# The tail of the last SSD group: the last y products in front of its four gate tiles, the norm's halves behind the second and the third

## The chip, the cores and the metric

The kernel runs on one core of one Trainium2 chip, as one program. The metric is the device time in microseconds of that core. Engines are named as in the profile: PE is TensorE's matmul, PEld its weight load, DVE is VectorE, ACT is ScalarE, POOL is GpSimd, SP is SyncE, which issues the DMAs. "L134" is line 134 of the kernel before; the lines up to 521 are the same in both versions.

## The reference, cut to what matters

One post-norm layer of a hybrid encoder on 512 tokens of width 1024, in float32. A combined projection makes, among others, z, x, B, C and dt for a bidirectional SSD branch, q, k and v for a dilated attention branch, and the logits of two gates. Both branches are projected, gated and merged:

```python
u = h @ w_in
z, xbc, dt_f_raw, dt_b_raw, q, k, v, gate_logits = jnp.split(u, ...)
y_ssd = ssd_branch(z, xbc, dt_f_raw, dt_b_raw, ...) @ w_proj_ssd
y_att = attention_branch(q, k, v) @ w_proj_attn
gates = jax.nn.sigmoid(gate_logits + b_gate).reshape(bsz, s, N_BRANCHES, D_MODEL)
mix = (gates[:, :, 0] * y_ssd + gates[:, :, 1] * y_att) @ w_out
h = layer_norm(alpha * h + mix, ln1_g, ln1_b)
```

The SSD branch has 4 groups of 8 heads of 64 channels. What matters here is its end, by group:

```python
y = y_f + y_b + d_skip[:, None] * xh
y = y.reshape(bsz, s, D_INNER) * jax.nn.silu(z)
yg = y.reshape(bsz, s, SSD_GROUPS, D_INNER // SSD_GROUPS)
yg = yg * lax.rsqrt(jnp.mean(jnp.square(yg), axis=-1, keepdims=True) + NORM_EPS)
return yg.reshape(bsz, s, D_INNER) * ssd_norm_w
```

A feed-forward sublayer follows.

## The kernel before, in words

Activations lie transposed: 128 channels on the partitions, 512 tokens along the free dimension. So the SSD output y is 16 tiles `ys[0..15]` of 128 x 512, four for each group. Large products are made in three passes of a split: a float32 operand is written as a high part (a cast to float32r on ACT) plus a low part (a subtraction on DVE), and `mm3` issues high x high, high x low, low x high (L134 to L136).

Weights come through a stream: a DMA on SP into one of three raw buffers (L87), the cast to `wh` on ACT (L108), the subtraction to `wl` on DVE (L109), two buffers of each. `ws.get()` hands out the next weight and prepares the one after it; casts and subtractions are issued with raised priority. A `wh` buffer comes free when PE has finished the tile before the one that runs.

The column tiles of the combined projection are tasks (`tile_task`, L288): 24 products of 128 x 128 with 128 x 512, then an eviction. Gate tiles "g0" to "g15" are evicted by ACT with a tanh (L314) and stored to DRAM by SP (L315).

In the SSD stage, `run` (L497) interleaves two generators by a budget of time: `ssd(g)`, the work of a group, and `bg(...)`, column tiles. This order is PE's own and is kept by hand (`manual_schedule` for PE); the other engines get their order from the framework's planner, which goes by priority, readiness and the tiles' buffers. In `ssd(g)` each pair of heads makes two masked matrices G on DVE (L462). The y products of a pair (`y_out`, L351) come one step later on PE: 8 products of G with x into `ps_y` (L358, 16 records in the profile), then yt on DVE (L360), an add on POOL (L361), the product with the gated z into `ys[j]` on DVE (L362), its square on ACT (L364), and a running sum of the squares on POOL (L366). The last pair of a group is left in `late` and is put out in the next group's start; for group 3 there is no next one.

The norm of a group, `norm(g)` (L335), is a generator in two halves. The first sums the squares over the channels by products with ones (`ps_ms`, L340), then takes the square root on ACT (L342; it needs a table of ACT that the tanh is not in) and the reciprocal on DVE (L343), into the small tile `rr`. The second spreads `rr` to all partitions by products (`ps_rr`, L347) and multiplies the group's four y tiles (L349 on DVE). Groups 0 to 2 have their norm inside the next group's `ssd`.

In group 3 there are 15 gate tiles, g1 to g15. The last four (`TAIL`), g12 to g15, are taken out of the interleaving and run behind it, with what is left of the group's y and norm between them (L522 to L529). Then the pools `sp` and `xp` of the SSD stage are closed (L530), and the projection stage opens its pools. `rr`, the x tiles, the squares and G lie in `sp`; the activations' split and the staging tiles of the gate stores lie in `xp`. The new right-side pools (for `yh`, the gates' loads and some attention tiles, `q` and `k` of the first pair among them) lie where `sp` was; the left-side ones (`mx`, `ap`, with `q` and `k` of the second pair) lie over `xp` as well. All 16 y tiles are split into `yh` (ACT, L560) and `yl` (DVE, L561), in order. The first projection tile (`ps_pa`, L134 to L136) takes y tiles 0 to 7; PE's order interleaves the projection with the attention branch, whose first scores (`ps_s`, L626) come after 18 products of the projection.

Of the kernel before, what the change touches and what calls it, by code (L numbers as in the profile page):

```python
# [43 lines left out]
def hybrid_layer_kernel(ctx: ExitStack, tc: tile.TileContext, t: dict, out: bass.AP):  # L44
# [103 lines left out]
    def ps_tile(tag, name, bufs):  # L148
        return psp.tile([P, 512], F32, name=name, tag=tag, bufs=bufs)
# [138 lines left out]
    def tile_task(kind, j):  # L288

        wh, wl = ws.get()  # L290
        ps = ps_tile("mm", f"ps_{kind}{j}", 3)
        for k in range(0, KT, 2):
            last_mm[0] = mm3(ps, [(wh[:, q * P:(q + 1) * P], wl[:, q * P:(q + 1) * P]) for q in (k, k + 1)], xs_hl[k:k + 2], k == 0, k == KT - 2)
            if k < KT - 2:
                yield QT
        evict(kind, j, ps)
        yield QT
# [29 lines left out]
    def bg(seq):  # L327
        for k, j in seq:
            yield from tile_task(k, j)
# [5 lines left out]
    def norm(g):  # L335

        sq = tail[g]
        ps = ps_tile("tp", f"ps_ms{g}", 3)
        for c in range(NCH):
            pe.matmul(ps[:, c:c + 1], sq[:, ch(c)], ones[:, 0:1], start=True, stop=True)  # L340
        rr = sp.tile([P, NCH], F32, name=f"rr{g}", tag="rr", bufs=1)
        act.activation(rr, ps[:, 0:NCH], AF.Sqrt, bias=epsv[:, 0:1], scale=1.0 / 512.0)  # L342
        dve.reciprocal(rr, rr)  # L343
        yield 6.0
        ps = ps_tile("tp", f"ps_rr{g}", 3)
        for c in range(NCH):
            pe.matmul(ps[:, ch(c)], rr[:, c:c + 1].to_broadcast([P, P]), ident, start=True, stop=True)  # L347
        for j in range(4 * g, 4 * g + 4):
            dve.scalar_tensor_tensor(ys[j], ys[j], vec[:, V_NW + j:V_NW + j + 1], ps, op0=ALU.mult, op1=ALU.mult)  # L349

    def y_out(g, pr, xt, ms, be, sqs):  # L351

        j = 4 * g + pr
        py = ps_tile("y", f"ps_y{j}", 2)
        for c in range(NCH):
            for hh in range(2):
                hs = slice((pr * 2 + hh) * HD, (pr * 2 + hh + 1) * HD)
                pe.matmul(py[hh * HD:(hh + 1) * HD, ch(c)], xt[c][:, hs], ms[hh][:, ch(c)], start=True, stop=True)  # L358
        yt = sp.tile([P, S], F32, name=f"yt{j}", tag="acc", bufs=2)
        dve.scalar_tensor_tensor(yt, fm["x", j], vec[:, V_DSK + j:V_DSK + j + 1], py, op0=ALU.mult, op1=ALU.add)  # L360
        pool.tensor_add(yt, yt, be[:, 0, :])  # L361
        dve.tensor_mul(ys[j], ys[j], yt)  # L362
        sq = sp.tile([P, S], F32, name=f"sq{j}", tag="sq", bufs=2)
        act.activation(sq, ys[j], AF.Square)  # L364
        if pr:
            pool.tensor_add(sq, sq, sqs[-1])  # L366
        sqs.append(sq)
        tail[g] = sq

    late = [None]  # L370
# [126 lines left out]
    def run(a, b, ta, tb):  # L497
        ua = ub = 0.0
        a, b = iter(a), iter(b)
        la = lb = True  # L500
        while la or lb:
            if la and (not lb or ua / ta <= ub / tb):
                try:
                    ua += next(a)
                except StopIteration:
                    la = False
            else:
                try:
                    ub += next(b)
                except StopIteration:  # L510
                    lb = False
# [6 lines left out]
    with tc.manual_schedule(engines={mybir.EngineType.PE}):  # L518
        for g in range(GROUPS):
            rest = len(mix[g]) - (TAIL if g == 3 else 0)  # L520
            run(ssd(g), bg(mix[g][:rest]), 86.5 if g else 93.5, 4 * QT * rest)
        nrm = norm(3)  # L522
        for n, (k, j) in enumerate(mix[3][rest:]):
            for _ in tile_task(k, j):
                pass
            if n == 0:
                y_out(*late[0])
            if n > 1:
                next(nrm, None)  # L529
    pa.close()  # L530

# [414 lines left out]
    for f in range(2):  # L946
# [21 lines left out]
        for c in range(2):  # L968
# [19 lines left out]
            for i in range(4):  # L988
# [5 lines left out]
                else:  # L994
                    n = 512 // len(pss[i])
# [72 lines left out]
```

## Time and profile before

| | |
|---|---|
| Median of 3 runs | 1033.44 us (1032.58 to 1034.84) |
| The profiled execution | 1033.47 us, span 1031.7 us |
| PE busy | 1017.8 us, 99% |
| DVE, ACT, POOL busy | 650.9, 501.7, 73.8 us |
| Mean granted TensorE clock | 0.997 |
| The tail with the four gate tiles on PE | 469.8 to 494.8 us of the span |

A row of a timeline gives start, duration, engine, line, operation, output and inputs, and in brackets the idle time of the engine before it with what ended it. Matmuls overlap: one is 0.39 us long and the next starts 0.23 us after it. A row of windows gives the stretch, its length, the busy time and the number of instructions of PE, PEld, DVE, ACT and POOL, the granted clock (1.00 is full), the share of the DMA engines and their rate in GB/s. A row of the waits gives who waited for whom, the total in us, how often, and the longest.

### The profile page before, as it was taken

Reading aid. Unit: us, or ns where it says so; the run is one execution under the profiler, and the core shown is the slowest. Engines: PE = TensorE matmul, PEld = TensorE weight load, DVE = VectorE, ACT = ScalarE, POOL = GpSimd, SP = SyncE. Lnnn points to the kernel's source line nnn. Section 1 sums busy time; section 2 is a strip of 40 time slices with the busy share of each in tenths; the row PEclk is TensorE's granted clock in tenths of the full one; section 3 lists DMA queues with packets and bytes.
Section 4 is the critical chain, followed back from the end, with each engine's and each line's share of the span. In section 5 each row is a group of like instructions: output and inputs, shape, how many; then the busy total and the mean of one; then the engine's idle time right before and its main releaser. Section 6 shows DMA issues by size and latency. Waiting matters only on the chain.

```text
span 1031.7 us, 13700 instructions
## 1 busy us (share of the span) xinstructions
PE 1017.8 (99%) x5169; PEld 843.1 (82%) x5169; DVE 650.9 (63%) x1035; ACT 501.7 (49%) x977; POOL 73.8 (7%) x66
## 2 busy tenths in 40 slices
PE   9999999999999999999899999999999999999997
PEld 7888888888878888888678788898888888888886
DVE  4296978689979996975786186744442324443346
ACT  4444877478758875764674353223432223433120
POOL 0000101221121022112000000000000000000000
PEclk9999999999999999999999999999999999999999
DMA  6445355425542554464753278212333333333322
GB/s 236 148 154 137 116 192 172 143 80 177 173 153 102 185 183 154 155 197 152 261 169 91 72 234 280 78 42 62 103 100 87 98 102 100 90 97 102 97 87 81
DMA packets 48449, 140.42 MB, mean 136 GB/s; under 512 B 6528, under 2 KB 7424, under 8 KB 48128
## 3 DMA queue, kind: packets, MB, share of 16 engines
q1 hardware_dynamic: 48240, 139.30, 42.5%
q8 instruction: 40, 0.66, 0.2%
q10 hardware_dynamic: 144, 0.26, 0.1%
q14 instruction: 25, 0.20, 0.1%
HBM read 128.25 MB, written 11.30 MB: 135 GB/s over the span
## 4 chain that ended last, share of the span: by engine, by line
PE 94%; DVE 3%; ACT 1%; DMA 1%; issue 1%; POOL 0%; DVEq 0%; ACTq 0%; POOLq 0%
PE ps_u L135 6%; PE ps_u L136 6%; PE ps_d L134 6%; PE ps_u L134 6%; PE ps_d L135 6%; PE ps_d L136 6%; PE ps_pa L134 3%; PE ps_g L134 3%; PE ps_pa L135 3%; PE ps_pa L136 3%; PE ps_g L136 3%; PE ps_g L135 3%; PE ps_z L134 3%; PE ps_z L135 3%; PE ps_z L136 3%; PE ps_x L134 3%
## 5 line engine op out<-in xcount | busy, mean ns | idle before, releaser
L109 DVE TENSOR_TENSOR wl<-wraw,wh 128x1024 fp32r<-128x1024 f32 (+1 forms) x165 | 201.0, 1222 | 239.0 <-ACT wh L108 234.2
L108 ACT CAST wh<-wraw 128x1024 fp32r<-128x1024 f32 (+1 forms) x165 | 171.2, 1041 | 266.5 <-PE ps_d L136 108.6
L135 PE MATMUL ps_u<-htl,wh 128*128 128x512 f32 (+1 forms) x288 | 105.3, 366 | 0.3 <-DVE htl L909 0.3
L134 PE MATMUL ps_u<-hth,wh 128*128 128x512 f32 (+1 forms) x288 | 105.3, 366 | 0.0
L136 PE MATMUL ps_u<-hth,wl 128*128 128x512 f32 (+1 forms) x288 | 105.2, 365 | 0.0
L135 PE MATMUL ps_d<-wl,fh 128*128 128x512 f32 (+1 forms) x272 | 102.5, 377 | 0.0
L134 PE MATMUL ps_d<-wh,fh 128*128 128x512 f32 (+1 forms) x272 | 102.4, 377 | 0.0
L136 PE MATMUL ps_d<-wh,fl 128*128 128x512 f32 (+1 forms) x272 | 102.4, 377 | 0.0
L135 PEld LDWEIGHTS ps_u<-htl,wh 128*128 128x128 f32 x288 | 54.3, 189 | 9.2 <-DVE htl L909 0.5
L134 PEld LDWEIGHTS ps_u<-hth,wh 128*128 128x128 f32 x288 | 54.2, 189 | 8.9 <-ACT hth L908 0.3
L136 PEld LDWEIGHTS ps_u<-hth,wl 128*128 128x128 f32 x288 | 54.3, 189 | 8.8
L136 PEld LDWEIGHTS ps_d<-wh,fl 128*128 128x128 f32 x272 | 51.2, 188 | 9.5
L134 PEld LDWEIGHTS ps_d<-wh,fh 128*128 128x128 f32 x272 | 51.2, 188 | 9.4
L135 PEld LDWEIGHTS ps_d<-wl,fh 128*128 128x128 f32 x272 | 51.2, 188 | 9.3
L134 PE MATMUL ps_pa<-yh,wh 128*128 128x512 f32 x128 | 52.9, 413 | 2.5 <-ACT yh L560 2.5
L135 PE MATMUL ps_pa<-yl,wh 128*128 128x512 f32 x128 | 50.8, 397 | 1.5 <-DVE yl L561 1.5
L134 PE MATMUL ps_g<-xh,wh 128*128 128x512 f32 x128 | 51.4, 401 | 0.0
L450 DVE SCALAR_TENSOR_TENSOR U<-bc,acr,U 128x128 f32<-128x128 f32 x128 | 45.8, 392 | 8.7 <-ACT U L448 8.7
L134 PE MATMUL ps_x<-xh,wh 128*128 128x512 f32 x128 | 50.9, 398 | 0.0
L134 PE MATMUL ps_z<-xh,wh 128*128 128x512 f32 x128 | 50.9, 398 | 0.0
L136 PE MATMUL ps_pa<-yh,wl 128*128 128x512 f32 x128 | 50.6, 396 | 0.0
L136 PE MATMUL ps_g<-xh,wl 128*128 128x512 f32 x128 | 50.0, 391 | 0.0
(262 smaller groups left out, 2184.2 us busy)
## 6 DMA issues: line engine op xcount, KB each, us to landing
wraw<-in_w_in_dram SPq DMA_DIRECT2D x68, 512.0 KB, 3.5
bc<-dr_acr SPq DMA_DIRECT2D x32, 512.0 KB, 4.2
wraw<-in_w_up_dram SPq DMA_DIRECT2D x32, 512.0 KB, 3.6
wraw<-in_w_dn_dram SPq DMA_DIRECT2D x32, 512.0 KB, 3.6
be<-dr_ear SPq DMA_DIRECT2D x32, 256.0 KB, 4.5
wraw<-in_w_ps_dram SPq DMA_DIRECT2D x16, 512.0 KB, 3.7
dr_gate<-g SPq DMA_DIRECT2D x16, 256.0 KB, 2.0
wraw<-in_w_out_dram SPq DMA_DIRECT2D x8, 512.0 KB, 4.5
```

Source lines behind the costliest of these rows:

```text
L108: act.copy(h[:, :width], r[:, :width])
L109: dve.tensor_sub(l[:, :width], r[:, :width], f32(h[:, :width]))
L134: pe.matmul(ps, lh, rh, start=(first and i == 0), stop=False)
L135: pe.matmul(ps, lh, rl, start=False, stop=False)
L136: ins = pe.matmul(ps, ll, rh, start=False, stop=(last and i == n - 1))
L450: dve.scalar_tensor_tensor(U[:, ch(c)], bcs[0][:, hh, ch(c)], acr[:, c, h:h + 1], U[:, ch(c)], op0=ALU.subtract, op1=ALU.min)
```

## The change

The order of the tail on PE was: g12, y products of the last pair, g13, g14, norm's first half, g15, norm's second half. It becomes: y products of the last pair, g12, g13, norm's first half, g14, norm's second half, g15. Nothing else is edited; the planner orders the other engines anew.

```diff
         for g in range(GROUPS):
             rest = len(mix[g]) - (TAIL if g == 3 else 0)
             run(ssd(g), bg(mix[g][:rest]), 86.5 if g else 93.5, 4 * QT * rest)
-        nrm = norm(3)
+        y_out(*late[0])
         for n, (k, j) in enumerate(mix[3][rest:]):
             for _ in tile_task(k, j):
                 pass
             if n == 0:
-                y_out(*late[0])
-            if n > 1:
+                nrm = norm(3)
+            if n in (1, 2):
                 next(nrm, None)
     pa.close()
```

## The prediction

> **What bounds the kernel now.** I read the busy shares first, then who waited for whom on PE, then the windows around the edited stage, then each engine's timeline there.
>
> ```profile
> PE 1017.8 (99%) x5169; PEld 843.1 (82%) x5169; DVE 650.9 (63%) x1035; ACT 501.7 (49%) x977; POOL 73.8 (7%) x66
> ```
> ```profile
> PE ps_pa L134 <- ACT yh L560: 2.5, 1, 2.5
> PE ps_pa L135 <- DVE yl L561: 1.5, 1, 1.5
> ```
>
> PE is the bound, so only time in which it stands or runs slowly can be won. Its two longest waits follow each other at one place: the first products of the projection (ps_pa), right behind the tail that is edited, wait for the split of y into yh (ACT) and yl (DVE).
>
> ```profile
> 464.07:469.77 5.70, 5.70 (x26) 4.53 (x25) 5.60 (x13) 2.98 (x6) 0.74 (x1) 1.00 0.53 178
> 469.77:475.30 5.53, 5.53 (x25) 4.32 (x23) 2.49 (x3) 2.23 (x4) 2.59 (x2) 1.00 0.29 97
> 475.30:476.33 1.03, 1.03 (x18) 0.86 (x17) 0.19 (x2) 1.03 (x2) 0.00 (x0) 1.00 0.66 255
> 476.33:487.34 11.01, 11.01 (x51) 9.12 (x49) 3.77 (x4) 2.80 (x4) 2.58 (x2) 1.00 0.64 192
> 487.34:488.15 0.81, 0.81 (x10) 0.81 (x8) 0.00 (x0) 0.80 (x1) 0.00 (x0) 1.00 0.00 0
> 488.15:493.73 5.58, 5.58 (x26) 4.59 (x26) 1.41 (x2) 2.41 (x5) 0.00 (x0) 1.00 0.67 214
> 493.73:494.78 1.05, 1.05 (x9) 0.86 (x7) 0.00 (x0) 1.03 (x2) 0.00 (x0) 1.00 0.98 357
> 494.78:499.87 5.09, 1.09 (x5) 0.67 (x4) 4.99 (x7) 5.08 (x9) 0.00 (x0) 1.00 0.55 186
> 499.87:503.52 3.65, 3.65 (x11) 2.71 (x10) 3.13 (x6) 3.65 (x8) 0.00 (x0) 0.53 1.01 374
> 505.00:520.00 15.00, 15.00 (x79) 11.12 (x79) 14.47 (x43) 7.05 (x22) 0.00 (x0) 1.00 0.63 211
> ```
> ```profile
> 497.31 0.51 PE L134 MATMUL ps_pa<-yh,wh 128*128 128x512 f32 x1 [2.52 <-ACT yh L560]
> 499.29 0.50 PE L135 MATMUL ps_pa<-yl,wh 128*128 128x512 f32 x1 [1.48 <-DVE yl L561]
> 505.00 1.03 PE L626 MATMUL ps_s<-k,q 64*128 64x192 f32 x8
> ```
>
> The windows (the columns are busy time of PE, PEld, DVE, ACT and POOL, then the clock, DMA share and rate) are PE's order as it stands: g11, g12, the last y products, g13 with g14, the mean squares (ms), g15, the norm's spread (rr), then 5.09 us with only 1.09 busy, then 3.65 us at a clock of 0.53. From the end of rr at 494.78 to the first scores at 505.00 lie 10.22 us and 18 projection products. A gate tile's 24 take 5.53 us, 0.230 each, so 18 cost 4.15: **6.07 us are lost here**, namely 2.52 and 1.48 of waiting, 3.65 - 9 x 0.230 = 1.58 of slow clock, and about 0.5 of refilling.
>
> ```profile
> 472.37 0.63 ACT L364 ACTIVATE sq<-y 128x512 f32<-128x512 f32 x1 [4.08 <-DVE y L362]
> 472.91 1.03 ACT L108 CAST wh<-wraw 128x1024 fp32r<-128x1024 f32 x1
> ...
> 487.35 1.05 ACT L108 CAST wh<-wraw 128x1024 fp32r<-128x1024 f32 x1 [3.80 <-issue]
> 488.31 0.68 ACT L314 ACTIVATE g<-ps_g,vec 128x512 f32<-128x512 f32 x1
> 489.01 1.28 ACT L342 ACT_TABLE_LOAD   x1
> 490.30 0.26 ACT L342 ACTIVATE rr<-ps_ms,epsv 128x4 f32<-128x4 f32 x1
> 493.70 1.04 ACT L108 CAST wh<-wraw 128x1024 fp32r<-128x1024 f32 x1 [3.14 <-PE ps_g L135]
> 494.76 1.28 ACT L314 ACT_TABLE_LOAD   x1
> 496.06 0.69 ACT L314 ACTIVATE g<-ps_g,vec 128x512 f32<-128x512 f32 x1
> 496.65 8.41 ACT L560 CAST yh<-y 128x512 fp32r<-128x512 f32 x16
> ```
> ```profile
> 467.75 0.69 DVE L462 TENSOR_TENSOR G<-G,U 128x512 f32<-128x512 f32 x1
> ...
> 469.50 0.74 DVE L360 SCALAR_TENSOR_TENSOR yt<-x,vec,ps_y 128x512 f32<-128x512 f32 x1
> 471.64 0.69 DVE L362 TENSOR_TENSOR y<-y,yt 128x512 f32<-128x512 f32 x1 [1.40 <-POOL yt L361]
> 473.98 1.49 DVE L109 TENSOR_TENSOR wl<-wraw,wh 128x1024 fp32r<-128x1024 f32 x1 [1.64 <-ACT wh L108]
> ...
> 490.60 0.18 DVE L343 RECIPROCAL rr<-rr 128x4 f32<-128x4 f32 x1 [0.94 <-ACT rr L342]
> 494.78 1.22 DVE L109 TENSOR_TENSOR wl<-wraw,wh 128x1024 fp32r<-128x1024 f32 x1 [4.00 <-PE ps_rr L347]
> 495.92 2.71 DVE L349 SCALAR_TENSOR_TENSOR y<-y,vec,ps_rr 128x512 f32<-128x512 f32 x4
> 498.56 7.05 DVE L561 TENSOR_TENSOR yl<-y,yh 128x512 fp32r<-128x512 f32 x9
> ```
>
> What makes yh late is ACT's queue: the weight cast that waits for g15 (3.14 us idle before it), a table load, g15's eviction, only then yh0. What makes yl late is DVE's: that cast's wl, the norm's four multiplies, then yl0. Yet the first 12 y tiles do not need the last norm:
>
> ```profile
> L349 DVE SCALAR_TENSOR_TENSOR y<-y,vec,ps_rr x8: 739/742/747, 325.5 to 422.6; 128x512 f32<-128x512 f32 x8
> ```
>
> The groups before had their multiplies by 422.6. So yh0 could have been cast in ACT's idle time; the planner's order kept it back. The reason I infer is the place of its buffer: the yh pool lies where pool sp was, and rr, whose last reader is the rr product, is the last tile of sp. SP's queue speaks for it:
>
> ```profile
> 490.11 0.41 SPq L579 DMA_DIRECT2D q<-dr_qk  x1
> ...
> 496.77 0.32 SPq L315 DMA_DIRECT2D dr_gate<-g  x1
> ...
> 498.12 0.42 SPq L579 DMA_DIRECT2D q<-dr_qk  x1
> ```
>
> The first q load, into a right-side pool like yh's, stands ahead of the g15 store; the second, into the pool over xp, whose last user is that store, stands behind it.
>
> **The change, part by part.** PE issues the same instructions in another order, so its sum from 469.77 to the projection stays 25.01 us (windows two to seven). No DMA is added, and no instruction of any engine.
>
> *Last y products, in front of g12.* On PE from 469.77 to 470.80. Their G is ready at 467.75 + 0.69 = 468.44, 1.33 us ahead, so no wait. Behind it yt15 (0.74), POOL's add, y15 (0.69), the square (0.63) and the second add follow the chain of y14.
>
> ```profile
> 470.32 1.29 POOL L361 TENSOR_TENSOR yt<-yt,be 128x512 f32<-128x512 f32 x1 [3.61 <-DVE yt L360]
> ```
>
> POOL does four adds of 1.29 from 470.32; DVE's wl and the squares between them stretch this to 475.7 at best, about 480 if yt15 stands behind the wl of 473.98 (475.2, then 0.74 + 1.29 + 0.69 + 0.63 + 1.29). ms comes at 470.80 + 5.53 + 5.5 = 481.8: covered. What could suffer is g13's weight split, at 473.98 to 475.47 for a tile that starts at 476.33; a square ahead of its cast shifts it by about 1 us and the third product of g13 needs it at 476.8. I take 0, ends 0 and 2.5 (all of y15's chain queued ahead).
>
> *Norm's first half, behind g13.* ms at 481.8 to 482.6. ACT's weight cast, eviction, table load and square root took 490.56 + 0.22 - 487.34 = 3.4 us until the reciprocal ended; now 485.2. rr is wanted at 488.15: 2.9 us spare, zero cost.
>
> *Second half, behind g14.* rr at 488.15 to 489.20, then g15 to 494.78. On DVE wl (1.14 until the next starts) from 489.2, the four multiplies 490.35 to 493.0: 2.9 us of work leave the gap and lie beside g15.
>
> *The pool.* With rr read by 489.20, sp is free a gate tile earlier, and I expect the yh casts and the q, k and bias loads to move up. ACT: cast 488.15 to 489.19, table load to 490.5, g14's eviction to 491.1, then yh at 8.41 / 16 = 0.53 each, seven by 494.78. DVE: yl from 493.0 at 7.05 / 9 = 0.78 each; PE wants one per 0.69. yl0 is 1.3 us early, but the wl of the second projection weight (after a cast that starts at 494.78) costs DVE 1.14 plus up to 1 of waiting, so yl3 to yl5 are 0 to 0.9 late; I take 0.5. This is what is late next. The DMAs moved up are three on SP's queue, 0.4 us of issue each; the weight load behind them is wanted four tiles later.
>
> *Sum.* 6.07 - 0.5 = 5.6 us. The attention stage has DVE at 14.47 of 15.00 busy; DVE's own chain moves up by 495.92 - 490.35 = 5.6, less that waiting of up to 1. I take 0.3 for it: **-5.3 us**, ends -6.1 (nothing late) and -4.2 (0.9 and 1 late). Against the profiled execution's 1033.47 (span 1031.7) this is 1028.2; the median of the runs, 1033.44, is the same to 0.03.
>
> **The rivals.** 0.2% of 1033 is 2.1 us, about what a measurement tells from no change.
>
> *A. The split stays behind g15's eviction.* If the planner's order has another reason, ACT does at 494.78: cast 1.05, eviction 0.6 (the table load now lies at g14's), yh0 0.6: first product at 497.1, yl0 0.7 later, second product at 497.75 instead of 499.29. That wins 1.5 us; with the clock kept, 3.1. Time 1030.3 to 1031.9. For it: ACT idled 3.14 us and yh0 did not come. Against: the q load. On the clock: the row shows 0.53 for 3.65 us after 4.0 us of standing. [...]
>
> *B. The square root falls behind work that waits for g14.* rr follows one tile behind ms as before, but if ACT's order puts the next cast and g14's eviction ahead of the square root, the reciprocal ends at 488.15 + 1.04 + 0.6 + 1.28 + 0.26 + 0.3 = 491.6. PE stands 3.45 us, g15 ends at 498.2, and cast, table load, eviction, yh0 and yl0 end at 502.4 instead of 499.25: 3.1 us slower, **1036.6**. It decides once the square root comes more than 2.9 us later than I have it. For: exactly cast and eviction stood ahead of it at 487.35. Against: those had waited for the tile before ms, and their like now waits for g13.
>
> *C. The gain is handed back in the attention stage,* where DVE is nearly full: PE would arrive earlier and wait for scores' maxima. For: the 14.47. Against: DVE's start moves as far as PE's, and PE shows no wait there now. Whole give-back: 1033.4; the change then does not do what it should.
>
> **How the numbers follow.** Forecast 0.68, its own range 1027.0 to 1029.7 (the ends 1027.4 and 1029.3, and 0.4 for runs that scatter); A 0.16, half of it beyond 0.2%; B 0.07; C and a stall at g13 that eats the gain 0.09. Faster 0.68 + 0.08 + 0.01 = 0.77, same 0.15, slower 0.08. The range takes the forecast's ends and A: 1027.0 to 1032.0.
>
> **What would show it.** Right: no PE wait for yh or yl above 1 us; clock 1.00 all through; yh casts on ACT from about 491, ahead of the last gate eviction; L349 from about 490; y products between g11 and g12; ps_s first at about 500. Wrong: yh0 still behind g15's eviction (A); a PE wait in front of rr (B); waits at ps_s or ps_pt (C); a wait of PE for G at 469.8 or for wl at g13.

## The result and the profile after

The changed kernel takes 1027.72 us (median of 6 runs, 1027.16 to 1028.11) against 1033.31 us before (6 runs, 1032.58 to 1034.84). The ratio is 0.9943, with an interval of 0.9930 to 0.9955: 5.6 us faster. The profiled execution took 1027.38 us, with a span of 1025.6 us; 1028.2 was forecast.

The page's busy line first, then the waits of PE after (the two rows left out are 0.3 us each, far from the tail):

```profile
PE 1016.2 (99%) x5169; PEld 842.0 (82%) x5169; DVE 651.5 (64%) x1035; ACT 501.5 (49%) x977; POOL 73.8 (7%) x66
```
```profile
PE ps_warm L188 <- DVE warm L185: 1.2, 1, 1.2
PE ps_g L136 <- DVE wl L109: 0.4, 1, 0.4
...
PE ps_pa L135 <- DVE yl L561: 0.2, 1, 0.2
```

The instruction counts are those of before, so nothing was added or saved; the 2.5 us wait for yh is gone, and 0.2 is left of the 1.5 for yl. PE's busy time fell by 1.6, as much as the slow clock had cost before (1.58): in that stretch of the kernel before, seven products in a row, from 500.24 on, lasted 0.63 or 0.64 us instead of 0.39. The windows of the tail's last part after (columns as before):

```profile
488.20:493.80 5.60, 5.60 (x29) 4.71 (x29) 4.85 (x7) 5.57 (x9) 0.00 (x0) 1.00 0.66 227
493.80:498.86 5.06, 4.84 (x21) 3.32 (x19) 4.78 (x7) 5.06 (x10) 0.00 (x0) 1.00 0.70 228
```

The clock is 1.00 through all of it, and the stretch ahead of the first scores, which had 1.09 busy of 5.09, has 4.84 of 5.06. PE's timeline, at the points that mark the stages:

```profile
469.36 1.09 PE L358 MATMUL ps_y<-G,xt 128*64 128x128 f32 x16
481.40 0.94 PE L340 MATMUL ps_ms<-tri,sq 128*128 128x1 f32 x8
494.16 0.39 PE L134 MATMUL ps_pa<-yh,wh 128*128 128x512 f32 x1
...
497.49 0.50 PE L135 MATMUL ps_pa<-yl,wh 128*128 128x512 f32 x1 [0.22 <-DVE yl L561]
498.86 1.03 PE L626 MATMUL ps_s<-k,q 64*128 64x192 f32 x8
```

From the tail's start to the first scores it was 505.00 - 469.77 = 35.23 us and is 498.86 - 469.36 = 29.50: 5.73 us won inside the tail. The tail also begins 0.41 us earlier in this execution; the order ahead of it is unchanged, and there one execution shows a wait of 0.8 for xt (L399) that the other has not, and the other the 0.4 for wl of the list above. That part is not the change's. Together they are the 6.1 us between the spans. ACT, DVE and SP after, in the same place:

```profile
484.36 0.26 ACT L342 ACTIVATE rr<-ps_ms,epsv 128x4 f32<-128x4 f32 x1
487.76 1.04 ACT L108 CAST wh<-wraw 128x1024 fp32r<-128x1024 f32 x1 [3.14 <-PE ps_g L135]
...
490.71 3.73 ACT L560 CAST yh<-y 128x512 fp32r<-128x512 f32 x7
494.35 1.05 ACT L108 CAST wh<-wraw 128x1024 fp32r<-128x1024 f32 x1
495.30 0.68 ACT L314 ACTIVATE g<-ps_g,vec 128x512 f32<-128x512 f32 x1
```
```profile
484.66 0.18 DVE L343 RECIPROCAL rr<-rr 128x4 f32<-128x4 f32 x1 [0.94 <-ACT rr L342]
488.84 1.22 DVE L109 TENSOR_TENSOR wl<-wraw,wh 128x1024 fp32r<-128x1024 f32 x1 [4.00 <-PE ps_rr L347]
489.99 2.71 DVE L349 SCALAR_TENSOR_TENSOR y<-y,vec,ps_rr 128x512 f32<-128x512 f32 x4
492.62 3.08 DVE L561 TENSOR_TENSOR yl<-y,yh 128x512 fp32r<-128x512 f32 x4
495.61 1.22 DVE L109 TENSOR_TENSOR wl<-wraw,wh 128x1024 fp32r<-128x1024 f32 x1
496.75 3.73 DVE L561 TENSOR_TENSOR yl<-y,yh 128x512 fp32r<-128x512 f32 x5
```
```profile
484.58 0.38 SPq L579 DMA_DIRECT2D q<-dr_qk  x1
...
490.84 0.32 SPq L315 DMA_DIRECT2D dr_gate<-g  x1
```

Seven yh casts run ahead of g15's eviction, where none did. The norm's multiplies lie beside g15. The first q load stands ahead of g14's store as well; before, it stood only ahead of g15's.

### The profile page after: what moved, and what is told of

It is laid out like the page before. It is cut to its first block, busy times and chain, and to the rows that moved or that the text cites. A ratio compares the mean times of both kernels' runs of the same rounds, so it can differ in the third digit from the quotient of the medians.

```text
span 1025.6 us, 13697 instructions
## 1 busy us (share of the span) xinstructions
PE 1016.2 (99%) x5169; PEld 842.0 (82%) x5169; DVE 651.5 (64%) x1035; ACT 501.5 (49%) x977; POOL 73.8 (7%) x66
## 4 chain that ended last, share of the span: by engine, by line
PE 90%; DVE 5%; ACT 2%; DMA 2%; issue 1%; POOL 0%; DVEq 0%; ACTq 0%; POOLq 0%
PE ps_u L135 6%; PE ps_u L136 6%; PE ps_d L136 6%; PE ps_u L134 6%; PE ps_d L134 6%; PE ps_d L135 6%; PE ps_pa L134 3%; PE ps_z L134 3%; PE ps_z L136 3%; PE ps_z L135 3%; PE ps_pa L135 3%; PE ps_pa L136 3%; PE ps_x L134 3%; PE ps_x L136 2%; PE ps_x L135 2%; PE ps_yo L481 2%
## 5 line engine op out<-in xcount | busy, mean ns | idle before, releaser
L135 PE MATMUL ps_u<-htl,wh 128*128 128x512 f32 (+1 forms) x288 | 105.3, 366 | 0.3 <-DVE htl L909 0.3
L134 PE MATMUL ps_u<-hth,wh 128*128 128x512 f32 (+1 forms) x288 | 105.3, 366 | 0.0
L135 PE MATMUL ps_d<-wl,fh 128*128 128x512 f32 (+1 forms) x272 | 102.5, 377 | 0.0
L134 PE MATMUL ps_d<-wh,fh 128*128 128x512 f32 (+1 forms) x272 | 102.4, 377 | 0.0
L135 PEld LDWEIGHTS ps_u<-htl,wh 128*128 128x128 f32 x288 | 54.3, 189 | 9.2 <-DVE htl L909 0.5
L134 PEld LDWEIGHTS ps_u<-hth,wh 128*128 128x128 f32 x288 | 54.2, 189 | 8.9 <-ACT hth L908 0.3
L135 PEld LDWEIGHTS ps_d<-wl,fh 128*128 128x128 f32 x272 | 51.2, 188 | 9.5
L134 PEld LDWEIGHTS ps_d<-wh,fh 128*128 128x128 f32 x272 | 51.2, 188 | 9.4
L134 PE MATMUL ps_pa<-yh,wh 128*128 128x512 f32 x128 | 52.1, 407 | 0.0
L134 PE MATMUL ps_g<-xh,wh 128*128 128x512 f32 x128 | 51.5, 402 | 0.0
L134 PE MATMUL ps_z<-xh,wh 128*128 128x512 f32 x128 | 50.9, 398 | 0.0
L134 PE MATMUL ps_x<-xh,wh 128*128 128x512 f32 x128 | 50.9, 398 | 0.0
L135 PE MATMUL ps_pa<-yl,wh 128*128 128x512 f32 x128 | 50.1, 392 | 0.2 <-DVE yl L561 0.2
```

The source lines that it names most:

```text
L134: pe.matmul(ps, lh, rh, start=(first and i == 0), stop=False)
L135: pe.matmul(ps, lh, rl, start=False, stop=False)
```

## The experiments

Two theories stood at first. P: the planner puts the split and the loads behind the last reader of pool `sp`, the rr product; the norm's earlier second half frees it. N: the gain is the norm's own work (square root, table load, multiplies) leaving the gap; the buffer plays no part. All ratios below are to the kernel before, on the same chip.

**One half at a time.** The norm alone is moved, the y products stay behind g12:

```diff
-            if n > 1:
+            if n in (1, 2):
                 next(nrm, None)
```

> Norm's two halves behind g13 and g14 as in the change, the last y products left behind g12. Theory P (the split into yh and yl moves up because the last reader of pool sp, the rr products, comes before g15): nearly the whole gain stays; the sum of squares ends at 482.4 and the mean squares want it at 481.8, so PE waits 0.5 to 0.6 us there, and g13 does not wait for its wl (0.4 in the changed kernel): 1027.7 to 1028.2. Theory N (the gain comes from norm's multiplies, reciprocal and table load leaving the gap, the place of the split does not matter): the same time. Theory Y (the early y products carry it): 1031 to 1033.4.

1027.54 us, ratio 0.9936 (0.9924 to 0.9949). The y products alone, in front of g12:

```diff
+        y_out(*late[0])
         for n, (k, j) in enumerate(mix[3][rest:]):
...
-            if n == 0:
-                y_out(*late[0])
```

> Last y products in front of g12, norm's halves left behind g14 and g15. P and N: no gain, the split waits as before: 1033.3, or 0.4 more where g13 waits for its wl as in the changed kernel (1033.3 to 1033.8). Y: 1027.7 to 1030.

1033.01 us, ratio 0.9994 (0.9986 to 1.0003). PE's waits of the second:

```profile
PE ps_pa L134 <- ACT yh L559: 2.5, 1, 2.5
PE ps_pa L135 <- DVE yl L560: 1.5, 1, 1.5
```

The two waits are the old ones, to the tenth. The whole gain is the norm's move. What the y move is good for shows in the first: there the mean squares have to wait for POOL's running sum, which in the full change they do not:

```profile
PE ps_ms L340 <- POOL sq L366: 0.4, 1, 0.4
```

In the time nothing of it shows (1027.54 against 1027.72).

**P against N.** The full change, with pool `sp` kept in use until g15's eviction: one column of g15's gate tile (kept in `gst`) is copied into a tile of `sp` that takes rr's place. Nothing reads the copy.

```diff
+        hold = sp.tile([P, 1], F32, name="hold", tag="rr", bufs=1)
+        pool.tensor_copy(hold, gst[0][:, 0:1])
     pa.close()
```

> The changed kernel, with one 128x1 copy on POOL that reads g15's evicted tile into a new tile of pool sp, so sp is held until g15 is evicted; norm stays where the change puts it. [...] N: no loss, 1027.7.

1031.25 us, ratio 0.9976 (0.9966 to 0.9986). Its ACT timeline with the copy on POOL, its PE timeline and windows:

```profile
494.25 1.04 ACT L108 CAST wh<-wraw 128x1024 fp32r<-128x1024 f32 x1 [3.32 <-PE ps_g L135]
495.20 0.68 ACT L314 ACTIVATE g<-ps_g,vec 128x512 f32<-128x512 f32 x1
495.78 8.41 ACT L564 CAST yh<-y 128x512 fp32r<-128x512 f32 x16
495.94 0.65 POOL L533 COPY hold<-g 128x1 f32<-128x1 f32 x1 [17.07 <-ACT g L314]
```
```profile
496.44 0.51 PE L134 MATMUL ps_pa<-yh,wh 128*128 128x512 f32 x1 [2.00 <-ACT yh L564]
497.21 0.50 PE L135 MATMUL ps_pa<-yl,wh 128*128 128x512 f32 x1 [0.26 <-DVE yl L565]
```
```profile
494.20:497.60 3.40, 1.14 (x5) 0.54 (x4) 2.17 (x3) 3.35 (x6) 0.65 (x1) 1.00 0.34 109
497.60:501.00 3.40, 3.40 (x10) 2.58 (x9) 2.98 (x5) 3.40 (x8) 0.00 (x0) 0.50 0.93 278
```

One small tile in `sp` puts all 16 casts behind g15's eviction again, with 3.32 us in which ACT does nothing, though the norm is early. So the buffer holds the split back. It does so through the order that the planner gives ACT, not by a wait while the kernel runs: the first cast starts at 495.78, ahead of the copy at 495.94 that keeps `sp` in use. This is also the prediction's rival A (1030.3 to 1031.9), made real: the norm's own work out of the gap wins 2.3 us (1033.52 for the kernel before, beside it), and the freed pool the other 3.5.

**The buffer alone.** The kernel before, with rr outside `sp`. The first try gave it a tile of its own in the constant pool:

```diff
-        rr = sp.tile([P, NCH], F32, name=f"rr{g}", tag="rr", bufs=1)
+        rr = const.tile([P, NCH], F32, name=f"rr{g}", tag="rr", bufs=1)
```

> The kernel before, with rr in the pool that stays open for the whole kernel instead of sp; PE's order is that of before. P: sp is free once the mean squares are read, in front of g15, so yh0 to yh4 and yl0 to yl4 are made beside g15; PE does not wait for yh0 or yl0, and waits up to 0.8 us at yl5, which stands behind the second wl and norm's four multiplies: 1028.0 to 1028.8. N: nothing changes, 1033.3.

1034.46 us, ratio 1.0007 (0.9998 to 1.0016): missed by 6 us. Yet the tail gained what was expected, as its PE timeline shows:

```profile
500.06 1.03 PE L626 MATMUL ps_s<-k,q 64*128 64x192 f32 x8
...
1026.22 0.27 PE L136 MATMUL ps_d<-wh,fl 128*128 128x256 f32 x1
```

The first scores come 4.9 us earlier than before (505.00), but the last product of the kernel comes 1.7 later (1024.52 before). The loss lies in later stages that the edit does not touch; the groups of instructions name the products of the feed-forward's first half. One of their three passes before, and here (the other two rose alike, from 389 to 395):

```profile
L134 PE MATMUL ps_u<-hth,wh 128*128 128x512 f32 x224 | 87.1, 389 | 0.0
```
```profile
L134 PE MATMUL ps_u<-hth,wh 128*128 128x512 f32 x224 | 88.6, 396 | 0.0
```

The new tile lies in the first pool of the left side, and every left tile after it moved by 32 B a partition. To keep all places, rr then went into columns of `epsv` that no one uses:

```diff
-        rr = sp.tile([P, NCH], F32, name=f"rr{g}", tag="rr", bufs=1)
+        rr = epsv[:, 4 + 4 * g:8 + 4 * g]
```

> The kernel before with rr in four spare columns of the constant tile epsv instead of pool sp: as the run with rr in the constant pool, but without the 32 bytes by which that moved every tile of the left side; PE's order is that of before. P (the buffer decides when the split starts): the tail gains what it gained there, scores at about 500.1 instead of 505.0, and nothing is lost later: 1028.3 to 1028.8. N (norm must leave the gap): 1033.3 to 1034.4.

1028.22 us, ratio 0.9948 (0.9935 to 0.9962), with the order of before. Its ACT and PE:

```profile
490.10 2.69 ACT L560 CAST yh<-y 128x512 fp32r<-128x512 f32 x5
493.34 1.05 ACT L108 CAST wh<-wraw 128x1024 fp32r<-128x1024 f32 x1 [0.55 <-PE ps_g L135]
```
```profile
499.05 0.50 PE L135 MATMUL ps_pa<-yl,wh 128*128 128x512 f32 x1 [0.96 <-DVE yl L561]
```

One wait of 0.96 is left, because the norm's multiplies still stand between the fifth and the sixth yl. P therefore holds without the change's order: the buffer of a tile of four columns brings 4.75 us (1032.97 beside it) of the 5.6, while the norm's own work, in the run that held `sp`, brought 2.3. The two overlap, since both shorten the same wait.

**What 32 B do.** The kernel before, with only an unused tile added to the constant pool, of 8, 16 or 32 columns, that is 32, 64 and 128 B a partition:

```diff
+    const.tile([P, 8], F32, name="pad")
```

> The kernel before with an unused tile of 32 bytes per partition in the constant pool, which moves all later tiles of the left side by 32 bytes and changes no instruction order. Theory L (a product whose two operands lie 32 bytes apart modulo 64 takes 0.231 instead of 0.2275 us or more; those with a left-side weight and a right-side activation, ps_pa and ps_u, get it): 1038 to 1041, the up products 395 ns long and 4.9 us more from the first of them to the last of the down products. Rival (the loss behind the tail with rr in the constant pool came from its other order of loads and casts): 1033.3.

> The kernel before with an unused tile of 64 bytes per partition in the constant pool. Theory L (what counts is the distance of a product's two operands modulo 64): no change, 1033.3, up products 389 ns. Rival (any move of the left side against the right costs): 1038 to 1041.

> The kernel before with an unused tile of 128 bytes per partition in the constant pool, after 32 and 64 bytes both cost 6 to 7 us. If the distance of a product's two operands counts modulo 128: no change, 1033.4, up products 389 ns. If modulo 256 or more, or if any move costs: 1038 to 1041. In the kernel before the distance of weight and activation is 0 modulo 512 for the up products and 256 for the projection, both at 389.

1039.99 us (ratio 1.0059, 1.0045 to 1.0073), 1039.91 (1.0066, 1.0049 to 1.0083) and 1039.22 (1.0064, 1.0047 to 1.0081). The 32 B reproduce the loss of the first try, and neither 64 nor 128 B brings the old speed back: the theory that the distance counts modulo 64 is not borne out, nor is modulo 128. Last, 128 B more on the left and 128 B less in `edge`, a tile at the right side's start that nothing reads, so that the right side moves with the left:

```diff
+    const.tile([P, 32], F32, name="pad")
...
-    edge.tile([P, 56], F32, name="edge")
+    edge.tile([P, 24], F32, name="edge")
```

> The kernel before with an unused tile of 128 B on the left side and the right side's first tile (never read) 128 B smaller, so that both sides lie 128 B further on and the distance between them is as before. If the distance of the two operands of a product decides, ps_u is back at 389 ns and the time is 1033.3 us. If the left operands' own place decides, ps_u stays at 392 to 396 ns and the time at 1039 to 1040.

1034.16 us, ratio 1.0005 (0.9996 to 1.0015). The same row of the groups for the kernel with 128 B on the left alone, and then for the one with both sides moved (the added line makes L134 L135):

```profile
L135 PE MATMUL ps_u<-hth,wh 128*128 128x512 f32 x224 | 88.4, 395 | 0.0
L135 PE MATMUL ps_g<-xh,wh 128*128 128x512 f32 x128 | 51.4, 401 | 0.0
```
```profile
L135 PE MATMUL ps_u<-hth,wh 128*128 128x512 f32 x224 | 87.2, 389 | 0.0
```

ps_u (hth on the right, wh on the left) slows when the left side moves alone and recovers when both do, and ps_g, with xh and wh both on the left, stays at the 401 of before. Neither operand's own place decides: the right side lies alike before and with 128 B on the left, the left side alike in the last two runs. As far as these runs go, what counts is how far apart the two lie. The means of ps_pa hide it, 416 in both runs, because behind the two old waits ten products in a row lasted 0.63 us instead of 0.39 in the profiled execution of the last one, and five in the other's; the medians do not, 395 and then 389.

**Rival B, made real.** The full change, with the square root issued behind g14's eviction on ACT (left out below: a third stop in `norm(3)` ahead of the square root, and `gev`, which keeps the eviction's instruction):

```diff
-            if n in (1, 2):
+            if n == 1:
+                next(nrm, None)
+            if n == 2:
+                with tc.issue_after(gev[0].ins):
+                    next(nrm, None)
                 next(nrm, None)
```

> The changed kernel with norm's square root issued on ACT behind g14's eviction (rival B of the prediction made on purpose). As priced there: 1036.6, with the split left behind g15. P: PE stands 3.45 us in front of the rr products (cast 1.04, eviction 0.6, table load 1.28, square root 0.26, reciprocal 0.3), but sp is still free before g15, so the split stays early and only that stop is added to the changed kernel, with up to 1.6 us of slow clock behind it: 1031.2 to 1032.8.

1032.7 us, ratio 0.9997 (0.9988 to 1.0006). Its waits, its windows from the stop on, and ACT and PE in it:

```profile
PE ps_rr L349 <- DVE rr L345: 3.4, 1, 3.4
```
```profile
487.20:490.51 3.31, 0.00 (x0) 0.03 (x1) 1.40 (x2) 3.28 (x5) 0.00 (x0) 1.00 0.28 93
490.51:494.10 3.59, 3.59 (x13) 3.20 (x14) 1.78 (x3) 3.59 (x8) 0.00 (x0) 0.54 0.95 323
```
```profile
490.05 5.28 ACT L567 CAST yh<-y 128x512 fp32r<-128x512 f32 x10
490.51 1.77 PE L349 MATMUL ps_rr<-tri,rr 128*128 128x128 f32 x8 [3.38 <-DVE rr L345]
```

PE stands 3.4 us and then runs 3.59 at a clock of 0.54, which loses some 1.6: together the 5.0 us between this and the changed kernel. But ten yh casts run from 490.05 on, ahead of g15's eviction, and the projection does not wait. The first cast starts before the rr products at 490.51 read rr. So here too the casts do not wait for the last reader of `sp` while the kernel runs; the pool plays its part in the planner's order. That fits the line that opens the pool of yh with `reuse_waits="tile"` (L554).

**The parts put together.** y products behind g12, mean squares behind the first quarter of g14, rr behind g14 and in `epsv` (by the line shown above):

```diff
-            for _ in tile_task(k, j):
-                pass
+            for q, _ in enumerate(tile_task(k, j)):
+                if (n, q) == (2, 0):
+                    next(nrm)
...
-            if n > 1:
+            if n == 2:
                 next(nrm, None)
```

> A version against the two small waits left: last y products behind g12, mean squares a quarter into g14, rr products behind g14, rr in the spare columns of epsv. P: the sum of squares is ready, g13's wl is not held up by y15, yl0 to yl4 are made beside g14 and g15; no wait over 0.2 us in the tail: 1027.0 to 1027.7, 0 to 0.6 below the changed kernel. Rival: DVE spends the same work in another order and a wait at yl5 takes the place: 1027.7 to 1028.3.

1026.93 us, ratio 0.9939 (0.9927 to 0.9952). No wait is left in the tail, and the first scores come at 498.21. It has the lowest median here, but its interval lies over that of the changed kernel; the 0.8 us between them are not shown.

## Why the prediction was right, point by point

- **The loss of 6.07 us ahead of the first scores.** Right. 5.73 of it came back, 5.6 was the sum before the allowance for the attention stage.
- **The inferred reason, the pool.** Right as a reason for the planner's order, and now shown from both sides: holding `sp` takes the early split away with the norm early (1031.25), and freeing it brings the split with the norm late (1028.22). It is not a wait in the run: yh0 started at 495.78 ahead of the copy that held `sp` (495.94), and with the late square root at 490.05 ahead of the rr products (490.51).
- **y products in front of g12, cost 0.** Right: no wait for G, and none of g13 for its weight. The 0.4 for wl in the list of waits lies at 449.41, ahead of the tail, as this row of the changed kernel's PE shows:

```profile
449.41 0.50 PE L136 MATMUL ps_g<-xh,wl 128*128 128x512 f32 x1 [0.36 <-DVE wl L109]
```

- **Norm's halves.** Counted from the y products, ms was forecast 12.0 us later, and came 481.40 - 469.36 = 12.04 later; the reciprocal's end was forecast at 15.4, and came at 484.84 - 469.36 = 15.48. rr followed g14 without a wait.
- **yh and the residual at yl.** Seven casts were forecast ahead of the second weight cast, and seven came. The residual 0.5 was right: from the first product to the scores it took 498.86 - 494.16 = 4.70 us for 18 x 0.230 = 4.14, so 0.56 are lost, at yl4 and behind it: the product that waited 0.22 starts 0.61 after the one before it, and the next 0.33 after that. The cause is the one named, DVE's wl for the second weight (495.61, then yl4 from 496.75).
- **0.3 for the attention stage.** Mis-sized: nothing was given back. The projection's second part begins 6.1 us earlier and the last product of the kernel too, as the rows of before and after show:

```profile
599.23 0.39 PE L134 MATMUL ps_pb<-ath,wh 128*128 128x512 f32 x1
...
1024.52 0.28 PE L136 MATMUL ps_d<-wh,fl 128*128 128x256 f32 x1
```
```profile
593.09 0.39 PE L134 MATMUL ps_pb<-ath,wh 128*128 128x512 f32 x1
...
1018.42 0.28 PE L136 MATMUL ps_d<-wh,fl 128*128 128x256 f32 x1
```

  The 6.1 us of both pairs hold the 0.4 from ahead of the tail. So rival C did not happen. The 0.5 us between 1028.2 and the median of 1027.72 have two parts: 0.16 by which the profiled execution of before lay over its median of 1033.31, which is chance, and 0.29 by which the medians lie further apart (5.59) than the 5.3 forecast, about the size of this term.
- **Rival A's price.** Right: 1030.3 to 1031.9 was given, 1031.25 measured. Its two ends hung on the clock. The lower one needed the clock kept through the stop, which was the author's estimate and which no run shows: in the run that held `sp`, a stop of 2.00 and 0.26 us was followed by 3.4 us at 0.50 (497.60 to 501.00). Why the run lies 0.65 below the other end stays open. PE did not stand all the time ahead of the slow stretch: in the 3.40 us before it, it was busy for 1.14. The kernel before shows the same: the 4.0 us of standing that the prediction names are two waits, 2.52 and 1.48, and in the 3.41 us ahead of the slow clock PE was busy for 1.08:

```profile
496.46:499.87 3.41, 1.08 (x4) 0.67 (x4) 3.31 (x6) 3.41 (x8) 0.00 (x0) 1.00 0.62 197
```

- **Rival B's price.** Wrong: 1036.6 given, 1032.7 measured. The stop was right (3.45 against 3.4). What failed is the step behind it, which put yh0 behind g15's eviction as in the old order. In the run it follows the square root, while PE stands: PE's order has the rr products, the last readers of `sp`, ahead of g15, and so, as I read it, the planner was free to put the split there. Against that, the price lacked the slow clock (0.54 for 3.59 us).

## What to carry to other kernels

When an engine idles ahead of work whose inputs are long there, look at its order and then for the buffer: here the planner put the work on a pool opened over a closed one behind the old pool's last reader, and that was a reader of a tile of four columns. Moving that last reader, or that tile, let seven and five casts run early. If the held work starts before the reader it was held for, as it did in two runs here, it was held by its place in the queue and not by a wait. And when an added tile costs time in stages it has no part in, compare the mean duration of one product there (here 395 or 396 ns against 389): the layout, not the schedule, may have changed.

## What the runs showed of the hardware

- Moving the left side alone, where wh lies, by 32, 64 or 128 B a partition made ps_u's 128x512 products 395 or 396 ns instead of 389, and the kernel 6.4 to 7.0 us longer; moving both by 128 B did not. From the first ps_u to the last ps_d it is 352.2 us before (672.3 to 1024.5), 357.1, 356.9 and 356.8 with 32, 64 and 128 B on the left, and 352.2 with both sides moved. Which distances are good stays open: of the shifts of 0, 32, 64 and 128 B against each other only 0 was.
- In the run that held `sp`, 2.00 and 0.26 us of standing, with 0.5 of work between, were followed by 3.4 us at a clock of 0.50: the stop was shorter than the slow stretch behind it. Around the 0.96 us wait of the run with rr in `epsv` the clock stayed at 1.00; the window there:

```profile
497.00:499.71 2.71, 1.75 (x7) 0.86 (x6) 2.60 (x5) 2.71 (x6) 0.00 (x0) 1.00 0.74 247
```

- Behind nearly the same two waits the slow stretch was not always as long. After 2.52 and 1.48 us the kernel before ran 3.41 us at 0.51 (499.87 to 503.28). After 2.52 and 1.49, with 128 B on the left, five products in a row lasted 0.63 us instead of 0.39, and after 2.52 and 1.43, with both sides moved, ten. From the second product of the projection to the first scores these two took 5.44 and 6.48 us, so that alone moved a profile by some 1.0 us; what decides it stays open.
